# First modulation with a buffer for each weight tile, and the first projections' weights behind them in four large tiles

## The chip, the cores and the metric

The kernel runs on one core of one Trainium2 chip. The metric is the device time of one launch in microseconds; the same program is launched several times and the median of the timed runs is what is compared.

## What is computed

One hybrid decoder block on 512 tokens of 1024 channels, in f32. The change lies in its first lines, `sh1` and `sc1`, and in what follows on them directly:

```python
mod = jax.nn.silu(c) @ w_ada[l] + b_ada[l]                  # (1024) @ (1024 x 6144)
sh1, sc1, gt1, sh2, sc2, gt2 = jnp.split(mod, N_MOD, axis=-1)
h = modulate(rms_norm(x, norm_mix[l]), sh1, sc1)
mix = token_mixer(h, positions, w_in[l], ...)
...
proj = h @ w_in                                             # q_a, kv_a, k_rope | rwkv_in | gate_logits
o_mla = mla_branch(q_a, kv_a, k_rope_raw, positions, ...)   # rotary positions inside
o_rwkv = rwkv7_branch(rwkv_in, ...)
...
x = x + gt1[:, None, :] * mix
h = modulate(rms_norm(x, norm_ffn[l]), sh2, sc2)
x = x + gt2[:, None, :] * peer_ffn(h, w_query[l], ...)
```

## The kernel before

The tokens are worked on in four blocks of 128 (`NB`), in three groups: block 0, block 1, blocks 2 and 3. Each goes through the RWKV projections (`shifted`, weights `w_b`), the recurrent core (`rwkv`), latent attention (`mla_pre`, `mla`, weights `w_a`, `w_u`) and the tail; the expert stage at the end streams all expert weights for blocks 2 and 3 and gathers single experts for blocks 0 and 1. The code is written as streams of steps; a scheduler puts the instructions of all of them into one fixed list for each engine, and each engine works its list strictly in that order. SP's list issues most loads, POOL's the loads `w_a` and `w_u` and the gathers.

Before block 0 can be projected, the first modulation must be known. Lines 342 to 357 make it: the columns `sh1` (i = 0, ends in `hB`) and `sc1` (i = 1, ends in `hA`) are each a sum over eight weight rows `w_ada` of 128x1024, weighted by the condition `sc`. VectorE adds the rows up into `part` (line 348 the first row, line 350 the other seven), eight small matmuls with a column of ones sum `part` over its partitions (`ps_mod`), and lines 354 to 357 add bias and norm. The rows come two in one load of 1 MB (line 344) into a ring of `GL` = 4 buffers, so loads five to eight wait until VectorE is done with the first four. `modulated` then makes the block's `hT` (line 329), on which all of PE's work hangs.

`normed` (lines 277 to 320) scales the block's tokens by their root mean square. `rotary` (lines 387 to 421) makes the sine and cosine tables (`rot`, `cs`, `sn`) with some 45 small VectorE instructions out of `posi` and a constant in `cst`; only attention needs them. `cst` (662.5 KB, the identity and masks) is loaded whole on ACT's queue at the start. `shifted` (line 490 loads, lines 514 and 516 shift) takes each `w_b` tile of 512 KB through a ring `w1` of two buffers. `ada_rows` adds up the other four modulation rows in the same way beside the mixing (`L299`, one instruction for a row of 512 KB), each behind its own load. `kT`, `vA` and `qT2` of attention stand in the `gl` ring behind the weights; `kT` and `qT2` are cleared by POOL (lines 523, 525).

Of the kernel before, what the change touches and what calls it, by code (L numbers as in the profile page):

```python
# [9 lines left out]
F32 = mybir.dt.float32  # L10
# [6 lines left out]
ALU = mybir.AluOpType  # L17
# [15 lines left out]
GL = 4  # L33
# [123 lines left out]
def _build(ctx, tc, nc, A, out):  # L157
# [19 lines left out]
    def bank(name, tag, bufs):  # L177
        return pp.tile([P, 512], F32, name=name, tag=tag, bufs=bufs)
# [57 lines left out]
    def mm(o, l, r, start=True, stop=True):  # L236
        PE.matmul(o, l, r, start=start, stop=stop)  # L237
# [11 lines left out]
    rows = mp.tile([P, NROW], F32, name="rows")  # L249
    posi = cp.tile([P, NB], I32, name="posi")  # L250
    nc.sync.dma_start(cols, A["cols"])
    nc.scalar.dma_start(cst, A["cst"])
    nc.scalar.dma_start(posi, A["pos"])

    def C(k):
# [2 lines left out]
    def col(k):  # L258
        return cols[:, COLS[k][0]:COLS[k][1]]
# [78 lines left out]
    part = [b4("part") for _ in range(2)]  # L338
    V.tensor_scalar(col("ba")[:, 8:], col("ba")[:, 8:], 1.0, None, op0=ALU.add)
    ps = bank("ps_mod", "po", 1)  # L340
    for i in range(2):
        for k2 in range(KT // 2):
            w = pe.tile([P, 2, D], F32, name="w_ada", tag="gl", bufs=GL)
            nc.sync.dma_start(w, A["w_ada"][i, 2 * k2:2 * k2 + 2].rearrange("k p d -> p k d"))
            for k in range(2):
                ck = sc[:, 2 * k2 + k:2 * k2 + k + 1]
                if k2 + k == 0:
                    V.tensor_scalar(part[i], w[:, k], ck, None, op0=ALU.mult)
                else:
                    V.scalar_tensor_tensor(part[i], w[:, k], ck, part[i], op0=ALU.mult, op1=ALU.add)  # L350
        for j in range(8):
            mm(ps[:, 8 * i + j:8 * i + j + 1], part[i][:, j * P:(j + 1) * P], ones)
        if i == 0:
            V.tensor_tensor(hB, ps[:, 0:8], col("ba")[:, :8], op=ALU.add)
        else:
            V.tensor_tensor(hA, ps[:, 8:16], col("ba")[:, 8:], op=ALU.add)
            V.tensor_tensor(hA, hA, col("norm_mix"), op=ALU.mult)

    hTb[0] = modulated(nx0, x0, psum_r)

# [25 lines left out]

    def rotary():
        posf = small("posf", NB)
        V.tensor_copy(posf, posi)
        t5 = u5("rot", [P, 5, n64])  # L390
        ang, rk_, y2, sy, cy = t5[:, 0], t5[:, 1], t5[:, 2], t5[:, 3], t5[:, 4]
        for b in range(NB):
# [95 lines left out]
    def load_w(name, src, w=w2):  # L488
        w = w(name)
        nc.sync.dma_start(w, src)  # L490
        return split(w, k=KT)
# [8 lines left out]
    def shifted(hT, js, make):  # L500
# [2 lines left out]
        c = len(js)  # L503
        ps = psum_w("ps_b")
        for q, j in enumerate(js):
            proj(ps, q * n, load_w("w_b", A["w_b"][j], w1), hT)
        pr = prt("pr", [P, c, n + 1])
        for q, j in enumerate(js):
            G.tensor_copy(pr[:, q, 0:1], carry[:, j:j + 1])
# [978 lines left out]
```

## Time and profile before

| what | value |
|---|---|
| median of 3 runs | 1925.5 us (1922.1 to 1932.53) |
| profiled execution | 1922.58 us |
| its span, first to last instruction | 1920.8 us |
| PE busy | 1719.6 us, 90% of the span |
| DVE busy | 1592.0 us, 83% |
| ACT / POOL busy | 699.4 / 425.4 us |
| PE in the first 50 us | 13.42 us |
| moved by DMA | 588.73 MB, 307 GB/s |

The profiled execution takes 1.8 us more than its span; all times of rows count from the span's start. PE is TensorE, DVE VectorE, ACT ScalarE, POOL GpSimd. An f32 matmul stands in the trace as two instructions, so a projection tile of eight matmuls is 16. "DMA" is the busy share of the core's 16 DMA engines.

### The profile page before, as it was taken

What the parts mean: (1) busy time and instruction counts of PE and PEld (TensorE: products, weight loads), DVE (VectorE), ACT (ScalarE), POOL (GpSimd) and SP (SyncE); (2) the same over time, 40 slices, a digit from 0 to 9 for tenths busy, and PEclk for the clock granted to TensorE, in tenths of its full rate; (3) what the DMA queues carried; (4) which work ended last, traced back from release to release, by engine and by line L of the source; (5) the groups of instructions that cost most, each with busy time, mean ns of one, the idle gap of its engine ahead of it and who ended that gap; (6) DMA issues with size and microseconds to landing.
All of it is one profiled execution on the core that took longest, in us unless ns stands there. A gap on an engine that the chain in (4) does not pass through costs nothing.

```text
span 1920.8 us, 30217 instructions
## 1 busy us (share of the span) xinstructions
PE 1719.6 (90%) x11002; PEld 1469.5 (77%) x11002; DVE 1592.0 (83%) x3655; ACT 699.4 (36%) x1727; POOL 425.4 (22%) x394
## 2 busy tenths in 40 slices
PE   2879999999889999999699979869999999999992
PEld 2667777678888698888388868757899988889992
DVE  6665436359768898888699999979999999999998
ACT  1234232421323232331131133335555555555551
POOL 1210000000322220222232213022332333333233
PEclk9989999999889999999899989979999999999996
DMA  7743755066987875789989879989999999999997
GB/s 301 271 147 121 255 177 188 12 208 200 359 332 251 317 254 197 282 295 362 363 316 351 312 290 320 303 311 404 391 404 415 415 415 413 415 413 415 410 373 281
DMA packets 146065, 588.73 MB, mean 307 GB/s; under 512 B 13806, under 2 KB 41710, under 8 KB 111356
## 3 DMA queue, kind: packets, MB, share of 16 engines
q1 hardware_dynamic: 76336, 284.08, 40.2%
q0 software_dynamic: 39360, 280.51, 37.9%
q10 hardware_dynamic: 30220, 22.22, 3.6%
q8 instruction: 86, 1.41, 0.3%
q14 instruction: 63, 0.52, 0.1%
HBM read 566.81 MB, written 19.94 MB: 305 GB/s over the span
## 4 chain that ended last, share of the span: by engine, by line
PE 34%; issue 30%; DVE 12%; DMA 12%; POOL 11%; ACT 1%; POOLq 0%; ACTq 0%; SPq 0%; DVEq 0%
POOL gl L1134 11%; DMA gl<-in_experts,ii 5%; PE ps_b L237 4%; PE ps_gt L237 4%; DMA w_b<-in_w_b 4%; PE ps_q L237 3%; PE ps_ap L237 2%; PE ps_z L237 2%; DVE acc L1145 2%; DVE gl L1138 2%; PE ps_y L237 2%; PE ps_M L237 1%; PE ps_m L237 1%; PE ps_s L237 1%; PE ps_G L237 1%
## 5 line engine op out<-in xcount | busy, mean ns | idle before, releaser
L1134 POOL DMA_INDIRECT gl<-in_experts,ii x256 | 369.8, 1445 | 1010.5 <-DVE acc L1145 716.2
L1138 DVE SCALAR_TENSOR_TENSOR gl<-gl,h2p 128x1024 f32<-128x1024 f32 x256 | 311.1, 1215 | 51.2 <-DMA gl<-in_experts,ii 50.7
L1145 DVE SCALAR_TENSOR_TENSOR acc<-gl,z,acc 128x1024 f32<-128x1024 f32 x256 | 326.4, 1275 | 12.2 <-ACT z L1140 7.3
L237 PE MATMUL acc<-vl,ch 128*128 128x512 f32 x512 | 204.3, 399 | 6.9 <-DVE vl L1170 6.7
L237 PE MATMUL acc<-vh,cl 128*128 128x512 f32 x512 | 204.2, 399 | 5.6 <-DVE cl L1170 5.4
L237 PE MATMUL ps_z<-hh,ul 128*128 128x256 f32 x704 | 199.4, 283 | 0.2 <-DVE ul L1170 0.2
L237 PE MATMUL ps_z<-hh,uh 128*128 128x256 f32 x704 | 199.5, 283 | 0.0
L237 PE MATMUL ps_z<-hl,uh 128*128 128x256 f32 x704 | 199.2, 283 | 0.0
L237 PE MATMUL acc<-vh,ch 128*128 128x512 f32 x512 | 196.5, 396 | 2.2 <-ACT ch L1169 1.9
L1139 ACT ACTIVATE z<-z 128x1 f32<-128x1 f32 x256 | 51.9, 203 | 367.6 <-DVE gl L1138 366.6
L237 PE MATMUL ps_z<-hf,u_raw 128*128 128x256 f32 x640 | 157.1, 390 | 8.4 <-ACT i1T L1246 8.4
L1170 DVE TENSOR_TENSOR vl<-v_raw,vh 128x1024 fp32r<-128x1024 f32 x128 | 155.9, 1218 | 3.5 <-ACT vh L1169 3.3
L237 PE MATMUL ps_gt<-hT,w_b 128*128 128x128 f32 x1024 | 136.5, 288 | 9.1 <-DMA w_b<-in_w_b 8.8
L237 PEld LDWEIGHTS ps_gt<-hT,w_b 128*128 128x128 f32 x1024 | 127.2, 201 | 15.4 <-DMA w_b<-in_w_b 6.2
L237 PE MATMUL ps_b<-hT,w_b 128*128 128x128 f32 x896 | 126.6, 290 | 13.2 <-DMA w_b<-in_w_b 11.7
L1169 ACT CAST vh<-v_raw 128x1024 fp32r<-128x1024 f32 x128 | 134.1, 1047 | 11.4 <-DMA v_raw<-in_dense 6.3
L237 PEld LDWEIGHTS ps_z<-hl,uh 128*128 128x128 f32 x704 | 135.1, 192 | 3.8
L237 PEld LDWEIGHTS ps_z<-hh,uh 128*128 128x128 f32 x704 | 134.7, 191 | 3.4
L237 PEld LDWEIGHTS ps_z<-hh,ul 128*128 128x128 f32 x704 | 134.7, 191 | 0.4 <-DVE ul L1170 0.4
L237 PEld LDWEIGHTS ps_z<-hf,u_raw 128*128 128x128 f32 x640 | 117.8, 195 | 21.9 <-ACT i1T L1246 8.6
L237 PEld LDWEIGHTS ps_b<-hT,w_b 128*128 128x128 f32 x896 | 115.0, 202 | 24.9 <-issue 13.9
L237 PE MATMUL ps_q<-h2T,w_q 128*128 128x128 f32 x1024 | 125.2, 277 | 1.3 <-DMA w_q<-in_w_query 0.9
(443 smaller groups left out, 3293.4 us busy)
## 6 DMA issues: line engine op xcount, KB each, us to landing
u_raw<-in_dense SPq DMA_DIRECT2D x128, 512.0 KB
v_raw<-in_dense SPq DMA_DIRECT2D x128, 512.0 KB
w_b<-in_w_b SPq DMA_DIRECT2D x90, 512.0 KB
w_q<-in_w_query SPq DMA_DIRECT2D x48, 512.0 KB
w_ada<-in_w_ada SPq DMA_DIRECT2D x32, 512.0 KB
G<-gd SPq DMA_DIRECT2D x13, 1024.0 KB
w_o<-in_w_o SPq DMA_DIRECT2D x24, 512.0 KB
w_out<-in_w_out SPq DMA_DIRECT2D x24, 512.0 KB
```

The lines of the kernel that those rows point to most:

```text
L237: PE.matmul(o, l, r, start=start, stop=stop)
L1134: G.indirect_dma_start(out=gl, out_offset=None, in_=A["experts"], in_offset=bass.IndirectOffsetOnAxis(ap=ii[:, s:s + 1], axis=0))
L1138: V.scalar_tensor_tensor(gl[:, :D], gl[:, :D], 1.0, h2, op0=ALU.mult, op1=ALU.mult, accum_out=z[:, 0:1])
L1139: S.activation(z[:, 1:2], z[:, 0:1], AF.Gelu_apprx_tanh)
L1145: V.scalar_tensor_tensor(acc, gl[:, D:], z[:, 1:2], acc, op0=ALU.mult, op1=ALU.add)
L1169: S.copy(hi, x)
L1170: V.tensor_tensor(lo, x, hi.bitcast(F32), op=ALU.subtract)
```

## The change

```diff
--- before.py
+++ after.py
@@ -249,7 +249,7 @@
     rows = mp.tile([P, NROW], F32, name="rows")
     posi = cp.tile([P, NB], I32, name="posi")
     nc.sync.dma_start(cols, A["cols"])
-    nc.scalar.dma_start(cst, A["cst"])
+    nc.scalar.dma_start(cst[:, :P], A["cst"][:, :P])
     nc.scalar.dma_start(posi, A["pos"])
 
     def C(k):
@@ -338,23 +338,40 @@
     part = [b4("part") for _ in range(2)]
     V.tensor_scalar(col("ba")[:, 8:], col("ba")[:, 8:], 1.0, None, op0=ALU.add)
     ps = bank("ps_mod", "po", 1)
+
+    rows_in = []
+    for _ in range(4):
+        t = pe.tile([P, 2, D], F32, name="w_ada", tag="gl", bufs=GL)
+        rows_in += [t[:, 0], t[:, 1]]
+    rows_in += [hTr("w_ada"), hTr("w_ada"), b4("w_ada"), pe.tile([P, D], F32, name="w_ada", tag="h2p", bufs=1),
+                pe.tile([P, D], F32, name="w_ada", tag="acc", bufs=1), w2("w_ada"), w2("w_ada"), w2("w_ada")]
     for i in range(2):
-        for k2 in range(KT // 2):
-            w = pe.tile([P, 2, D], F32, name="w_ada", tag="gl", bufs=GL)
-            nc.sync.dma_start(w, A["w_ada"][i, 2 * k2:2 * k2 + 2].rearrange("k p d -> p k d"))
-            for k in range(2):
-                ck = sc[:, 2 * k2 + k:2 * k2 + k + 1]
-                if k2 + k == 0:
-                    V.tensor_scalar(part[i], w[:, k], ck, None, op0=ALU.mult)
-                else:
-                    V.scalar_tensor_tensor(part[i], w[:, k], ck, part[i], op0=ALU.mult, op1=ALU.add)
-        for j in range(8):
-            mm(ps[:, 8 * i + j:8 * i + j + 1], part[i][:, j * P:(j + 1) * P], ones)
+        for k in range(KT):
+            w = rows_in[KT * i + k]
+            nc.sync.dma_start(w, A["w_ada"][i, k])
+            if i == 1 and k == KT - 1:
+                for j in range(8):
+                    c = ps[:, 8 * i + j:8 * i + j + 1]
+                    mm(c, part[i][:, j * P:(j + 1) * P], ones, True, False)
+                    mm(c, w[:, j * P:(j + 1) * P], sc[:, k:k + 1], False, True)
+            elif k == 0:
+                V.tensor_scalar(part[i], w, sc[:, k:k + 1], None, op0=ALU.mult)
+            else:
+                marks["ada"] = V.scalar_tensor_tensor(part[i], w, sc[:, k:k + 1], part[i], op0=ALU.mult, op1=ALU.add)
         if i == 0:
-            V.tensor_tensor(hB, ps[:, 0:8], col("ba")[:, :8], op=ALU.add)
-        else:
-            V.tensor_tensor(hA, ps[:, 8:16], col("ba")[:, 8:], op=ALU.add)
-            V.tensor_tensor(hA, hA, col("norm_mix"), op=ALU.mult)
+            for j in range(8):
+                mm(ps[:, 8 * i + j:8 * i + j + 1], part[i][:, j * P:(j + 1) * P], ones)
+    with tc.issue_after(marks["ada"].ins):
+        V.tensor_tensor(hB, ps[:, 0:8], col("ba")[:, :8], op=ALU.add)
+    V.tensor_tensor(hA, ps[:, 8:16], col("ba")[:, 8:], op=ALU.add)
+    V.tensor_tensor(hA, hA, col("norm_mix"), op=ALU.mult)
+    w_first = {}
+    for j in (12, 0, 4, 8):
+        t = pe.tile([P, 2, D], F32, name="w_b2", tag="gl", bufs=GL)
+        nc.sync.dma_start(t, A["w_b"][j:j + 2].rearrange("k p d -> p k d"))
+        for k in range(2):
+            w_first[j + k] = split(t[:, k], k=KT)
+    nc.sync.dma_start(cst[:, P:], A["cst"][:, P:])
 
     hTb[0] = modulated(nx0, x0, psum_r)
 
@@ -386,7 +403,8 @@
 
     def rotary():
         posf = small("posf", NB)
-        V.tensor_copy(posf, posi)
+        with tc.issue_after(marks["ada"].ins):
+            V.tensor_copy(posf, posi)
         t5 = u5("rot", [P, 5, n64])
         ang, rk_, y2, sy, cy = t5[:, 0], t5[:, 1], t5[:, 2], t5[:, 3], t5[:, 4]
         for b in range(NB):
@@ -503,7 +521,7 @@
         c = len(js)
         ps = psum_w("ps_b")
         for q, j in enumerate(js):
-            proj(ps, q * n, load_w("w_b", A["w_b"][j], w1), hT)
+            proj(ps, q * n, w_first.pop(j) if j in w_first else load_w("w_b", A["w_b"][j], w1), hT)
         pr = prt("pr", [P, c, n + 1])
         for q, j in enumerate(js):
             G.tensor_copy(pr[:, q, 0:1], carry[:, j:j + 1])
```

In words: every `w_ada` row of the first modulation has a buffer (eight in the four `gl` buffers, the rest in tiles that are free at that time, three of them the `w2` buffers into which `w_a` is loaded later) and a load of its own of 512 KB; the last row is not added by VectorE but multiplied by eight more matmuls on PE. `hB` is placed behind the last addition. Only the identity part of `cst` (64 KB) is loaded at first, the rest later on SP. The weights `w_b` 12 and 13, 0 and 1, 4 and 5, 8 and 9 (block 0's first projections) are loaded in four loads of 1 MB into the `gl` buffers right behind `w_ada`. The conversion that `rotary` starts with is placed behind the last addition.

What this does to the engines' lists follows. SP's list before, from its start (`hT<-in_x` are tokens of a block):

```order
L251 DMA cols<-in_cols 128x84
L308 DMA hT<-in_x 128x1024
L344 DMA w_ada<-in_w_ada 128x2x1024 x8
L368 DMA rows<-in_rows 128x448
L370 DMA w_up<-in_w_up 128x512
L372 DMA w_gu<-in_w_gate_up 128x512
L374 DMA sk<-in_sk 128x256
L490 DMA w_b<-in_w_b 128x1024 x2
L308 DMA hT<-in_x 128x1024
```

SP's list after, from its start:

```order
L251 DMA cols<-in_cols 128x84
L308 DMA hT<-in_x 128x1024
L351 DMA w_ada<-in_w_ada 128x1024 x16
L371 DMA w_b_190<-in_w_b 128x2x1024
L371 DMA w_b_192<-in_w_b 128x2x1024
L371 DMA w_b_194<-in_w_b 128x2x1024
L371 DMA w_b_196<-in_w_b 128x2x1024
L374 DMA cst<-in_cst 128x1197
L385 DMA rows<-in_rows 128x448
L387 DMA w_up<-in_w_up 128x512
```

The four double `w_b` loads now stand between the last `w_ada` row and `rows`, `w_up`, `w_gu`, `sk`; the loads of line 490 that follow begin eight tiles later in the order of use.

DVE's list before, from the second modulation row to its end (`rot`, `cs` and `sn` are rotary's):

```order
L348 TENSOR_SCALAR part<-w_ada,sc 128x1024
L408 TENSOR_SCALAR rot<-rot 128x64
L420 TENSOR_SCALAR cs<-cs 128x4x16
L350 SCALAR_TENSOR_TENSOR part<-w_ada,sc,part 128x1024
L407 TENSOR_TENSOR rot<-rot 128x64
L421 COPY cs<-cs 128x4x16
L408 TENSOR_SCALAR rot<-rot 128x64
L417 SCALAR_TENSOR_TENSOR sn<-rot 128x4x16
L418 TENSOR_SCALAR sn<-sn 128x4x16
L350 SCALAR_TENSOR_TENSOR part<-w_ada,sc,part 128x1024 x6
L356 TENSOR_TENSOR hA<-ps_mod,cols 128x8
L357 TENSOR_TENSOR hA<-hA,cols 128x8
```

DVE's list after at the same place (line 360 is the old 350, 358 the old 348):

```order
L289 SCALAR_TENSOR_TENSOR rs<-rst,rs 128x1
L360 SCALAR_TENSOR_TENSOR part<-w_ada,sc,part 128x1024
L320 TENSOR_SCALAR hT<-hT,rs 128x1024
L360 SCALAR_TENSOR_TENSOR part<-w_ada,sc,part 128x1024 x5
L358 TENSOR_SCALAR part<-w_ada,sc 128x1024
L360 SCALAR_TENSOR_TENSOR part<-w_ada,sc,part 128x1024 x6
L407 CAST posf<-posi 128x4
L365 TENSOR_TENSOR hB<-ps_mod,cols 128x8
L366 TENSOR_TENSOR hA<-ps_mod,cols 128x8
L367 TENSOR_TENSOR hA<-hA,cols 128x8
```

No rotary instruction stands between the additions any more, `hB` no longer stands between the two halves, and there are 13 long additions in place of 14. In DVE's list after, the rotary instructions now begin behind the r projection's shift (line 534 is the old 516), go around the k projection's shift and `kk`, and end at the v projection's shift and the norm of `kk` (`ssk`):

```order
L532 TENSOR_TENSOR sh<-pr 128x256
L534 SCALAR_TENSOR_TENSOR sh<-sh,cols,pr 128x128 x2
L1077 CAST iota_255<-cst 128x128
L411 TENSOR_SCALAR rot<-cst,posf 128x16 x4
...
L532 TENSOR_TENSOR sh<-pr 128x256
L425 TENSOR_TENSOR rot<-rot 128x64
L534 SCALAR_TENSOR_TENSOR sh<-sh,cols,pr 128x128 x2
L719 TENSOR_SCALAR kk<-sh,cols 128x128 x2
...
L439 COPY cs<-cs 128x4x16
L426 TENSOR_SCALAR rot<-rot 128x64
L532 TENSOR_TENSOR sh<-pr 128x256
L726 TENSOR_SCALAR ssk<-ps_ss 128x4
```

The rows left out there are rotary's, some 45 in all. Behind them, up to the scaled tokens of block 1 (`hT`, the old line 320), DVE's list after has eleven line 299 additions; the list before has seven between the v projection's shift and that same instruction.

PE's list before, from the modulation's matmuls (`ps_b` are block 0's projections, `ps_qa` attention's, `ps_up` the decay's):

```order
L237 MATMUL ps_mod<-ones,part 128x1 x16
L237 MATMUL ps_qa<-w_a,hT 128x416
L237 MATMUL ps_b<-hT,w_b 128x128 x8
L237 MATMUL ps_qa<-w_a,hT 128x416
L237 MATMUL ps_b<-hT,w_b 128x128 x8
L237 MATMUL ps_up<-sh,w_up 128x128 x2
L237 MATMUL ps_qa<-w_a,hT 128x416
L237 MATMUL ps_up<-sh,w_up 128x128 x2
L237 MATMUL ps_qa<-w_a,hT 128x416 x2
L237 MATMUL ps_b<-hT,w_b 128x128 x16
L237 MATMUL ps_qa<-w_a,hT 128x416 x3
```

PE's list after at the same place:

```order
L237 MATMUL ps_mod<-ones,part 128x1 x9
L237 MATMUL ps_mod<-sc,w_ada 128x1
L237 MATMUL ps_mod<-ones,part 128x1
...
L237 MATMUL ps_mod<-sc,w_ada 128x1
L237 MATMUL ps_qa<-w_a,hT 128x416
L237 MATMUL ps_b<-hT,w_b_190 128x128 x8
L237 MATMUL ps_qa<-w_a,hT 128x416
L237 MATMUL ps_b<-hT,w_b_190 128x128 x8
L237 MATMUL ps_qa<-w_a,hT 128x416
L237 MATMUL ps_b<-hT,w_b_192 128x128 x16
L237 MATMUL ps_qa<-w_a,hT 128x416
L237 MATMUL ps_b<-hT,w_b_194 128x128 x16
```

The modulation's sixteen matmuls became 24, the projections run through their first 64 matmuls with little between, and the decay's `ps_up` went behind three of the four double tiles. Further back, attention's first keys and queries of block 0 (`ps_kq` of `w_uq`, `ps_qkT`) moved behind the first steps of the recurrent core, and by PE's 600th of some 8300 instructions the lists agree again to the end.

## Rows read from the trace of the kernel before

**Rows 1.** The page, parts 1 and 2: engines over the span, PE by slice.

```profile
PE 1719.6 (90%) x11002; PEld 1469.5 (77%) x11002; DVE 1592.0 (83%) x3655; ACT 699.4 (36%) x1727; POOL 425.4 (22%) x394
PE   2879999999889999999699979869999999999992
```

**Rows 2.** Stretches of 50 us: columns, the first, one of the last stage.

```profile
core 0: us, PE busy (x) PEld busy (x) DVE busy (x) ACT busy (x) POOL busy (x), PEclk, DMA share, GB/s
0.00:50.00 50.00, 13.42 (x55) 12.13 (x56) 29.36 (x85) 5.72 (x14) 9.29 (x18) 1.00 0.75 289
1450.00:1500.00 50.00, 49.96 (x319) 45.13 (x318) 50.00 (x66) 27.94 (x56) 13.08 (x10) 1.00 1.02 415
```

**Rows 3.** Waits, 0 to 48 us: total, times, longest us.

```profile
ACT hT L329 <- DVE hA L357: 36.5, 1, 36.5
```

**Rows 4.** DMA from 0 to 110 us: GB/s in 40 slices of 2.75 us.

```profile
GB/s 19 384 414 412 408 407 410 410 410 410 349 343 419 264 1 0 110 80 25 243 305 393 399 301 352 247 277 378 240 302 358 252 162 127 398 116 317 198 133 198
```

**Rows 5.** Timeline of the first modulation: start, us, engine, instruction [idle before].

```profile
7.30 0.60 ACT L317 ACTIVATE ps_sqr<-hT 128x512 f32<-128x512 f32 x1 [2.91 <-DMA hT<-in_x]
12.28 0.75 DVE L348 TENSOR_SCALAR part<-w_ada,sc 128x1024 f32<-128x1024 f32 x1 [1.18 <-DMA w_ada<-in_w_ada]
28.37 0.17 DVE L354 TENSOR_TENSOR hB<-ps_mod,cols 128x8 f32<-128x8 f32 x1 [3.29 <-PE ps_mod L237]
30.79 1.92 DVE L421 COPY cs<-cs 128x64 f32<-128x64 f32 x1
30.84 1.81 POOL L523 MEMSET kT<- 32x2048 f32 x1 [26.42 <-DMA w_ada<-in_w_ada]
33.15 7.88 DVE L350 SCALAR_TENSOR_TENSOR part<-w_ada,sc,part 128x1024 f32<-128x1024 f32 x6
41.09 3.57 PE L237 MATMUL ps_mod<-ones,part 128*128 128x1 f32 x16 [12.75 <-DVE part L350]
45.69 1.75 PE L237 MATMUL ps_qa<-w_a,hT 128*128 128x416 f32 x2 [1.04 <-ACT hT L329]
47.24 3.62 PE L237 MATMUL ps_b<-hT,w_b 128*128 128x128 f32 x16
51.97 1.95 PE L237 MATMUL ps_b<-hT,w_b 128*128 128x128 f32 x16
```

**Rows 6.** Stretch 12.2 to 24.8 us, rotary instructions alone: DVE busy, clock, DMA.

```profile
12.20:24.80 12.60, 3.34 (x22) 1.00 1.03 409
```

**Rows 7.** Stretches after the modulation, columns as in rows 2.

```profile
65.60:69.00 3.40, 3.37 (x16) 3.40 (x17) 1.62 (x11) 0.00 (x0) 0.24 (x2) 0.51 0.95 349
45.60:77.90 32.30, 27.15 (x159) 22.59 (x159) 18.96 (x47) 8.31 (x28) 6.64 (x19) 0.95 0.79 270
77.90:127.40 49.50, 39.18 (x234) 31.58 (x232) 39.65 (x129) 16.13 (x45) 6.62 (x20) 0.93 0.56 185
127.40:183.20 55.80, 51.64 (x314) 40.01 (x315) 27.63 (x104) 22.95 (x71) 5.44 (x15) 0.97 0.38 118
```

**Rows 8.** Waits of PE, 45 to 183 us.

```profile
PE ps_b L237 <- DMA w_b<-in_w_b: 8.1, 4, 2.7
PE ps_qa L237 <- DMA w_a<-in_w_a: 1.9, 1, 1.9
```

**Rows 9.** Waits of DVE, 45.6 to 127.4 us.

```profile
DVE part L299 <- DMA w_ada<-in_w_ada: 6.2, 4, 3.2
```

**Rows 10.** Line 299 from 77.9 to 127.4 us: ns min/median/max, starts.

```profile
L299 DVE SCALAR_TENSOR_TENSOR part<-w_ada,sc,part x7: 1267/1276/1285, 79.7 to 124.8; 128x1024 f32<-128x1024 f32 x7
```

**Rows 11.** Three stretches ahead of the v projection's shift: DVE busy, clock, DMA.

```profile
56.30:59.40 3.10, 2.90 (x7) 1.00 0.93 318
65.20:67.60 2.40, 1.99 (x12) 0.57 0.94 317
74.40:76.40 2.00, 1.86 (x9) 1.00 1.03 412
```

**Rows 12.** Timeline of DVE: the v projection's shift.

```profile
77.94 0.43 DVE L514 TENSOR_TENSOR sh<-pr 128x256 f32<-128x256 f32 x1
```

## The prediction

> **What bounds the kernel now.** I read the page first. PE is busy for 90% of the span, and its slices are full except at the very start [rows 1]; in the last stage PE and DVE are busy for nearly the whole of each 50 us and DMA moves 415 GB/s, but in the first 50 us PE works for 13.42 us [rows 2]. Nothing later has an appointed time: what the start loses, everything behind it loses. So I looked at the waits of the start. ACT waits 36.5 us for `hA` before it can make `hT` [rows 3], though DMA moves some 410 GB/s from 5.5 us on [rows 4]. In the timeline DVE gets its first row at 12.28 us, gets `hB` only at 28.37 after 3.29 us idle for PE, does the last six additions in 7.88 us, 1.31 each, PE then multiplies for 3.57 us, and at 45.69 us the first projection begins [rows 5]. DVE is the bound of this stage: besides the rows it carries 22 rotary instructions (3.34 us) between 12.2 and 24.8 [rows 6]. Behind it, PE from 45 to 183 us waits 8.1 us for `w_b` loads and 1.9 for `w_a` [rows 8]. DVE is 80% busy between 77.9 and 127.4 (39.65 of 49.5 us) and half busy around that [rows 7].
>
> **The change part by part.** The times count from the start of the span.
>
> *Loads.* Ahead of the first row stood 42 KB, 662.5 KB of `cst`, 512 KB of tokens, 1248 KB of `w_a` in parallel, and the row comes in a pair of 1 MB: 3.57 MB, which by the slices of [rows 4] had moved at 11.5 us; DVE starts 0.8 later. Now it is 42 + 64 + 512 + 512 KB = 1.16 MB, moved by 5.6 us; with the same 0.8 it lands at 6.4. A further row is 0.524 MB at 410 GB/s, 1.28 us: the fifteenth lands at 24.3, the sixteenth at 25.6. No load waits for DVE any more. The double `w_b` tiles follow by 28, 31, 33 and 36 us, shared with two of `w_a` by 35. The parts of `cst` and `w_up` that come later land by about 42, before their readers.
>
> *DVE.* The tokens land some two microseconds earlier than the 7.30 of [rows 5], so the squares (two of 0.60 with their read-outs) are done at about 6.5 and DVE starts at 6.9. Its list is two first rows at 0.75, thirteen additions at 1.31, nine small instructions of the norm at 0.2 and the scaling, 0.74: 21.0 us, end at 27.9. That is later than the fifteenth row's landing, so DVE remains the bound, by 3.6 us, and a somewhat slower load costs nothing. Against 41.03 it is 13.1 us earlier: 5.4 by the first landing, 3.3 by `hB`, 1.3 by the row given to PE, the rest by rotary.
>
> *The row given to PE.* Sixteen matmuls stand behind the last addition in place of eight: 7.1 us by the 3.57 for eight [rows 5]. It saves an addition of 1.31 and costs 3.57, a loss of 2.3. PE ends at 35.0; with `hB` now behind it, the first projection starts 1.2 us later, 36.2, **9.5 us earlier** than 45.69. If PE's clock rises on the way, up to half of the 7.1 could be saved; bounds 32.7 to 36.2.
>
> *Block 0's projections.* From 45.6 to the v projection's shift at 77.94 [rows 12] it is 32.3 us before. The first 16 instructions of `ps_b` took 3.62 us, the next 16 1.95 [rows 5]: at half speed, 1.2 GHz, as in the stretch at a granted 0.51 [rows 7], though the record shows 1.00 there. I take the same slow 6.2 us at first (two `ps_qa`, 16 `ps_b`), then 112 instructions of `ps_b` at 0.122 less overlap, 13.1, 2.8 of `ps_qa` and `ps_up`, and 0.6 for the copy and shift: 22.7 us, since these tiles are there and the waits of [rows 8] in this part are gone. **9.6 us saved**, 19 in all, shift done at 58.9. Rotary now lies in this part, some 45 instructions of 0.15 us by [rows 6], 7 us; DVE was busy for 18.96 of 32.3 us here [rows 7], much of it the decay's work and `L299`, which now come later, and it waits for projections in between. I cost it at nothing; without that cover it is 7 us.
>
> POOL's three clears of `kT` and `qT2` come in this part too. Beside one of them, 1.81 us, a copy of 64 elements took 1.92 us on DVE [rows 5]; three would hold DVE for at most 5.4. DVE has room for that here, so I cost it at nothing too.
>
> *What is given back.* From 77.94 to block 1's scaled tokens at 127.3, DVE's list grows. Of what was done before the v projection's shift, three pieces now come after it: the decay's scan and reciprocal (2.90 us busy), the key norm of attention with one product (1.99), and attention's scaled keys (1.86) [rows 11]; three of rotary's (0.4) and four more `L299` at 1.28 [rows 10] as well: 12.3 us. So 39.65 busy becomes 51.9. With no idle time it is 51.9, with the 9.85 idle of before 61.8; I take half, 57, since a fuller engine idles less but the chain of norms, PE and back stays: **7.5 us lost** on 49.5, bounds 2.4 to 12.3. Behind that, to 183 us, two heads of attention more are left (2.2 us of PE) and the wait for `w_a` (1.9) falls away, as those loads are issued earlier; 28 us of DVE are free there [rows 7]. From there the lists are the same and everything shifts.
>
> **Sum.** 9.5 + 9.6 - 7.5 - 0.3 = 11 us. On the profiled execution's 1922.58 that is 1911.6. The median of the runs is 2.9 higher, so I say 1914.5.
>
> *A rule on load sizes.* In the last stage weights come in loads of 512 KB too, and DMA moves 415 GB/s there [rows 2]. The Trainium skill, "DMA: Bandwidth & Descriptors", section Bandwidth, wants loads of at least 1 MiB and gives 341 GB/s for a single one of that size; at that rate (my estimate from that page) the sixteenth row would land at 29.5 us and cost 1.5 of the gain. No run here shows a single load by itself; the row with many in flight speaks against a loss.
>
> **The rivals.**
>
> *Most of it stays.* DVE idles little between the shift and block 1 (51.9 us, 5 more kept) and PE's clock is up early (3.5): 19 to 20 us, 1905. For it speaks that DVE idles 9.85 us there now; against it, that PE and DVE answer each other in that stretch.
>
> *The lead is given back.* DVE's longer list has the idle time of before (61.8 us, 4.8 less) and rotary or the clears meet the k projection's shift (up to 7): 0 to 6 us left, 1922. What speaks for it is that DVE is the fullest engine there and that `L299` additions stand ahead of the second norm in its list.
>
> *Late rows.* If the rows came at 243 GB/s, as one slice of [rows 4] shows, a row would take 2.16 us, the sixteenth would land at 38.8, PE would begin the projections at about 46 and the start's lead would be gone; then 9.6 - 7.8 = 2 us remain: 1923. The slices at the time of these loads are at 410, and that one is from later, so this is unlikely.
>
> *Slower.* `L299` stands in DVE's one list and each waits for its own load, which SP issues behind loads that wait for PE. Before, four waits cost 6.2 us, the longest 3.2 [rows 9]. Eleven now stand where DVE is full. At 3.2 each it takes four to eat the 11 us and seven (22 us) to end over 0.5% slower, about 1937. That is double the rate of before.
>
> **Chances and range.** Forecast (gain 6 to 15) 0.58; most stays 0.13; given back 0.15; late rows 0.05; slower 0.09. Half a per cent, 9.6 us, is about what a measurement of this kernel can tell from no change (the three runs spread over 10 us). Of the forecast's 0.58 some 0.37 lie beyond it. So faster 0.50, same 0.41, slower 0.09. The range goes from the rival with the largest gain, less a little for the spread, 1901, to 1926, where the lead is given back and the spread adds 4; about 0.15 to 0.2 is left outside.
>
> **What would show it.** In the changed profile: the first row's product at about 7 us, additions back to back to about 28, `ps_mod` with 32 instructions in 5 to 7 us, the first `ps_qa` near 36; no PE wait for `w_b` until the first group's last tiles; the v projection's shift near 59, block 1's scaling near 116, and from PE's attention to block 1 on a constant lead. Wrong would be: the additions waiting for loads, rotary between k's projection and its norm holding PE, `L299` waits over 6 us, or a lead that shrinks behind 183 us.

## The result and the profile after

The changed kernel takes 1907.93 us (median; 1900.54 to 1917.77) against 1925.5. The ratio is 0.9926, interval 0.9898 to 0.9954: 0.74% or 14 us faster (the two medians lie 17.6 us apart). The forecast was 1914.5 us, with faster by over half a per cent as the likeliest case. The profiled execution has a span of 1906.2 us, 14.6 less than before.

The page and two stretches of 50 us, which answer to [rows 1] and [rows 2]:

```profile
PE 1720.0 (90%) x11018; PEld 1472.0 (77%) x11018; DVE 1587.9 (83%) x3654; ACT 699.8 (37%) x1727; POOL 437.2 (23%) x394
PE   5879999999899999999699979779999999999992
```

```profile
0.00:50.00 50.00, 27.41 (x153) 24.99 (x154) 25.64 (x56) 7.26 (x19) 10.33 (x29) 1.00 0.99 387
1450.00:1500.00 50.00, 50.00 (x323) 45.61 (x322) 49.62 (x65) 28.35 (x56) 18.83 (x10) 1.00 1.02 415
```

PE does twice the work of before in the first 50 us; the last stage is what it was. The start in the timeline, as [rows 5], with the v projection's shift [rows 12] and the scaling of block 1:

```profile
6.65 0.74 DVE L358 TENSOR_SCALAR part<-w_ada,sc 128x1024 f32<-128x1024 f32 x1
11.84 6.56 DVE L360 SCALAR_TENSOR_TENSOR part<-w_ada,sc,part 128x1024 f32<-128x1024 f32 x5
27.05 0.59 PE L237 MATMUL ps_mod<-ones,part 128*128 128x1 f32 x2 [5.01 <-DVE part L360]
34.07 0.17 DVE L365 TENSOR_TENSOR hB<-ps_mod,cols 128x8 f32<-128x8 f32 x1 [7.00 <-PE ps_mod L237]
35.12 1.75 PE L237 MATMUL ps_qa<-w_a,hT 128*128 128x416 f32 x2 [1.08 <-ACT hT L329]
36.67 3.18 PE L237 MATMUL ps_b<-hT,w_b 128*128 128x128 f32 x16
39.68 0.86 PE L237 MATMUL ps_qa<-w_a,hT 128*128 128x416 f32 x2
56.66 0.41 DVE L532 TENSOR_TENSOR sh<-pr 128x256 f32<-128x256 f32 x1
112.00 0.75 DVE L320 TENSOR_SCALAR hT<-hT,rs 128x1024 f32<-128x1024 f32 x1
```

No addition waits for a row. The first projection begins at 35.12 instead of 45.69, the shift comes at 56.66 instead of 77.94, the scaling begins at 112.0 instead of 126.6: leads of 10.6, 21.3 and 14.6 us. The scaling before:

```profile
126.57 0.75 DVE L320 TENSOR_SCALAR hT<-hT,rs 128x1024 f32<-128x1024 f32 x1
```

DMA in 40 slices of 2.75 us, as [rows 4], moves 407 to 423 GB/s while the 512 KB rows come, up to some 27 us, and 383 to 420 behind them up to 41 us, with the double tiles:

```profile
GB/s 81 337 423 413 410 413 414 407 407 408 420 399 413 408 383 406 397 417 335 27 6 52 259 341 285 334 343 204 195 310 73 0 159 68 123 191 0 193 308 191
```

Waits of PE from 35 to 171 us ([rows 8]) and one of DVE from 36 to 125 ([rows 9]):

```profile
PE ps_qkT L631 <- DVE qk L627: 8.0, 1, 8.0
PE ps_b L237 <- DMA w_b<-in_w_b: 3.7, 2, 2.1
PE ps_ss L237 <- ACT sq L720: 2.4, 1, 2.4
```

```profile
DVE part L299 <- DMA w_ada<-in_w_ada: 2.1, 2, 1.1
```

The waits for weights have shrunk from 8.1 us to 3.7, but a single wait of 8.0 for attention's q, which DVE makes, is new. What stands around it (columns as in [rows 2]):

```profile
56.66:112.00 55.34, 39.60 (x219) 30.83 (x218) 47.24 (x159) 15.57 (x46) 7.79 (x21) 0.84 0.53 181
112.00:170.80 58.80, 55.04 (x333) 43.01 (x334) 32.61 (x113) 25.92 (x79) 4.95 (x15) 0.95 0.42 139
108.00:112.00 4.00, 0.00 (x0) 0.00 (x0) 3.98 (x12) 0.00 (x0) 0.00 (x0) 0.50 0.28 114
112.00:116.00 4.00, 3.77 (x17) 3.39 (x18) 1.43 (x4) 1.72 (x4) 0.00 (x0) 0.50 0.38 131
```

The granted clock is 0.50, 1.2 GHz, at the end of that wait and for the 4 us of work behind it. In the whole stretch from shift to scaling its mean is 0.84; before it was 0.93 [rows 7].

**Where the lead goes.** I take two marks: A, the first `ps_qa`, and T, the first `ps_tok` of the later group (183.1 us before, 170.8 after), behind which PE's lists of before and after differ in seven rows only, and from some 230 us in none. T before and after:

```profile
183.10 0.27 PE L758 MATMUL ps_tok<-cst,AR 128*128 128x128 f32 x1
```

```profile
170.84 0.28 PE L776 MATMUL ps_tok<-cst,AR 128*128 128x128 f32 x1
```

A is 10.57 earlier, T 12.3. From A to T:

```profile
45.69:183.10 137.41, 117.86 (x705) 94.08 (x706) 86.24 (x280) 47.20 (x143) 18.69 (x53) 0.95 0.54 178
```

```profile
35.12:170.80 135.68, 116.18 (x700) 92.73 (x701) 90.22 (x327) 47.52 (x142) 21.89 (x56) 0.91 0.53 184
```

The first row is of before, the second of after. PE idles 19.5 us in both: one wait took the other's place. Up to the shift PE, idle for 5.1 us before, now never is; from the shift to T it idles 5.0 us more than before and works 4.0 us more (first row after, up to the shift; then before and after from the shift to T):

```profile
35.12:56.66 21.54, 21.54 (x150) 18.89 (x151) 10.38 (x57) 6.03 (x19) 9.15 (x21) 1.00 0.82 315
```

```profile
77.94:183.10 105.16, 90.67 (x548) 71.49 (x547) 67.28 (x233) 38.98 (x116) 12.01 (x35) 0.95 0.46 149
```

```profile
56.66:170.80 114.14, 94.64 (x552) 73.84 (x552) 79.85 (x271) 41.49 (x125) 12.74 (x36) 0.90 0.48 159
```

Behind T the lead over before, by the same ACT instruction in both traces, goes to 8.2 us at 280, 11.2 at 400, 12.6 at 1000 and 14.8 at the end. One place of this drift is taken up below; the rest isn't explained.

### The profile page after: what moved, and what is told of

Read it like the earlier page. It is cut to its first block, busy times and chain, and to the rows that moved or that the text cites. A ratio compares the mean times of both kernels' runs of the same rounds, so it can differ in the third digit from the quotient of the medians.

```text
span 1906.2 us, 30258 instructions
## 1 busy us (share of the span) xinstructions
PE 1720.0 (90%) x11018; PEld 1472.0 (77%) x11018; DVE 1587.9 (83%) x3654; ACT 699.8 (37%) x1727; POOL 437.2 (23%) x394
## 3 DMA queue, kind: packets, MB, share of 16 engines
q1 hardware_dynamic: 76544, 284.69, 40.4%
## 4 chain that ended last, share of the span: by engine, by line
issue 31%; PE 31%; DVE 13%; POOL 12%; DMA 11%; ACT 1%; POOLq 0%; SPq 0%; ACTq 0%; DVEq 0%
POOL gl L1152 12%; DMA gl<-in_experts,ii 5%; PE ps_b L237 4%; PE ps_gt L237 4%; DMA w_b<-in_w_b 3%; PE ps_q L237 3%; DVE acc L1163 3%; PE ps_z L237 2%; DVE gl L1156 2%; PE ps_ap L237 2%; PE ps_y L237 1%; PE ps_m L237 1%; PE ps_G L237 1%; PE ps_M L237 1%; PE ps_s L237 1%
## 5 line engine op out<-in xcount | busy, mean ns | idle before, releaser
L1152 POOL DMA_INDIRECT gl<-in_experts,ii x256 | 382.9, 1496 | 989.1 <-DVE acc L1163 697.0
L1163 DVE SCALAR_TENSOR_TENSOR acc<-gl,z,acc 128x1024 f32<-128x1024 f32 x256 | 326.6, 1276 | 12.6 <-ACT z L1158 7.1
## 6 DMA issues: line engine op xcount, KB each, us to landing
G<-gd SPq DMA_DIRECT2D x13, 1024.0 KB, 10.6
```

The source lines that it names most:

```text
L1152: G.indirect_dma_start(out=gl, out_offset=None, in_=A["experts"], in_offset=bass.IndirectOffsetOnAxis(ap=ii[:, s:s + 1], axis=0))
L1163: V.scalar_tensor_tensor(acc, gl[:, D:], z[:, 1:2], acc, op0=ALU.mult, op1=ALU.add)
```

## The experiments

Each was run with the kernel before on the same chip; the ratio is to that. The edits are to the changed kernel, unless said otherwise.

**e1_vrow, the last row back on VectorE.**

```diff
-            if i == 1 and k == KT - 1:
-                ... (the 16 matmuls)
-            elif k == 0:
+            if k == 0:
...
-        if i == 0:
-            for j in range(8):
+        for j in range(8):
```

> The changed kernel with the last modulation row added by VectorE again (14 long additions, 16 small matmuls in all). Theory (the row given to PE is a loss on the path that sets the end of the modulation): one addition more, 1.3 us, and eight matmuls less, 3.4 us, so the first ps_qa begins at 33.0 us instead of 35.1, the v projection's shift comes at 54.5 instead of 56.7, and the end is about 2 us earlier. Rival (TensorE's clock decides): the longer run of small matmuls is what lets the clock rise early in the projections; then the first ps_qa still begins at 33.0, but the low clock lasts as much longer, the shift comes at 56 to 57 and the end does not move. Second rival (the last row is late): the last addition waits for its load, and the first ps_qa begins at 35 or later.

```profile
29.19 3.58 PE L237 MATMUL ps_mod<-ones,part 128*128 128x1 f32 x16 [6.36 <-DVE part L355]
```

The first `ps_qa` begins at 33.85 (35.12 after; 35.9 in e4_late299, which has the same start and ran on this chip). So the row on PE does cost 1.3 to 2 us there. But the ratio is 0.9973 (0.9946 to 1.0), slower than the changed kernel's. The small edit also reordered all lists: PE's agrees with that of the changed kernel only from its 1157th instruction on, some 380 us in. The end can't be put down to the row alone; e6_vrow_cst was made for that.

**e2_ring, without the double tiles.**

```diff
-    for j in (12, 0, 4, 8):
+    for j in ():
```

> The changed kernel without the four double weight tiles: the first projections' weights go through the ring of two buffers as before. Theory (the projections were waiting for their weights): the first ps_qa stays at 35 us, the v projection's shift comes 9 to 10 us later, at 66, PE waits for w_b again (6 us or more up to there), and of this up to 6 us comes back by block 1's scaling, since VectorE does the decay's work in the longer wait; the end is 4 to 9 us later. Rival (the projections were short of clock, not of weights): the shift comes within 3 us of 56.7 and the end within 3 us of the changed kernel.

First `ps_qa` 35.63, scaling 124.5, ratio 0.9967 (0.9941 to 0.9992), some 8 us behind the changed kernel, as the theory said. The v projection's shift comes at 71.59 and not at 66:

```profile
71.59 0.42 DVE L532 TENSOR_TENSOR sh<-pr 128x256 f32<-128x256 f32 x1
```

That is 14.9 us late; of this 2.4 has come back at the scaling (12.5 late) and 4.0 at T (10.9 late). From A to T:

```profile
35.63:181.70 146.07, 126.56 (x705) 100.39 (x706) 93.03 (x322) 47.12 (x143) 16.57 (x53) 0.87 0.52 177
```

PE idles 19.5 us again. Its busy time for the same matmuls is 10.4 us more than in the changed kernel, at a mean clock of 0.87.

**e3_rot, constants whole at the start and rotary early.**

```diff
-    nc.scalar.dma_start(cst[:, :P], A["cst"][:, :P])
+    nc.scalar.dma_start(cst, A["cst"])
...
-    nc.sync.dma_start(cst[:, P:], A["cst"][:, P:])
...
-        with tc.issue_after(marks["ada"].ins):
-            V.tensor_copy(posf, posi)
+        V.tensor_copy(posf, posi)
```

> The changed kernel with the constants loaded whole at the start and the rotary tables placed where the scheduler puts them, as before. Theory (VectorE bounds the modulation): 0.6 MB more ahead of the first row, 1.5 us, and 22 or more rotary instructions of 0.15 us between the additions, 3.3 us or more, so the first ps_qa begins at 40 us (39 to 42) and the v projection's shift at 61.5, as rotary lay beside the projections without cost; nothing of it comes back later, and the end is 4 to 5 us later. Rival (rows bound the modulation, rotary lies in the waits): first ps_qa at 36.6 or less, the end within 2 us. Second rival (rotary beside the projections did cost): the stretch from first ps_qa to the shift becomes shorter than 21.5 us by 2 us or more and gives that back.

First `ps_qa` at 41.63, 5.7 later than in e4_late299, as expected, and the shift at 62.37: rotary beside the projections was free. The ratio is 1.0036 (1.0011 to 1.0062), some 21 us behind the changed kernel and not 4 to 5. As in e1_vrow, PE's list differs up to some 380 us, so how much of this loss is rotary's isn't shown.

**e4_late299, the additions of line 299 behind block 1's scaling.**

```diff
-        V.scalar_tensor_tensor(part, w, sc[:, k:k + 1], part, op0=ALU.mult, op1=ALU.add)
+        with tc.issue_after(marks["x1"].ins):
+            V.scalar_tensor_tensor(part, w, sc[:, k:k + 1], part, op0=ALU.mult, op1=ALU.add)
...
-        V.tensor_scalar(x, x, rs, None, op0=ALU.mult)
+        marks[f"x{b}"] = V.tensor_scalar(x, x, rs, None, op0=ALU.mult)
```

> The changed kernel with all line 299 additions held behind the scaling of block 1's tokens: eleven of 1.28 us (14 us) leave VectorE's stretch between the v projection's shift (56.7) and that scaling (112.0) and come behind it, where VectorE is a little over half busy. Theory (VectorE's list is the bound of this stretch and is what gave back 6 of the 21 us): the scaling comes 7 us earlier, at 105 (103 to 108), PE's wait for attention's q (8.0 us) shrinks by 2.5 us or more; the end is 3 to 7 us earlier, if the stretch behind has room for the 14 us. Rival (the stretch is a chain through PE and ACT, and the additions lie in its gaps): the scaling stays within 2 us of 112 and the end too. Second rival (it only moves the load): the scaling is earlier, but the lead is gone by 220 us and the end is the same or later.

The scaling comes at 102.9, 9 us earlier, and PE's wait for q is 5.8: VectorE's list is what holds that stretch. But the ratio is 0.9959 (0.9935 to 0.9983). Behind it the additions then stand ahead of other work and wait for their own loads; waits of DVE up to 260 us, from 103 in e4_late299 and, second, from 112 in the changed kernel:

```profile
DVE part L300 <- DMA w_ada<-in_w_ada: 30.5, 11, 6.3
```

```profile
DVE part L299 <- DMA w_ada<-in_w_ada: 21.0, 9, 4.6
```

The second rival: the load was moved, and the lead over the changed kernel is gone by 160 us. Here too PE's list differs, from 66 to some 380 us. By the same ACT instructions the two profiles then stay within some 5 us of each other, either way, and are level at 1000 us; the 8.5 us of loss at the end of this profile come behind, where the lists agree, and their cause isn't shown. Of the 14.2 us that e1_vrow's profile loses on the changed kernel's, 10 come behind 1000 us in the same way.

From here on I chose edits whose lists stay those of the changed kernel from about PE's 600th instruction on.

**e5_posf, the hold on rotary's first conversion taken away.**

```diff
-        with tc.issue_after(marks["ada"].ins):
-            V.tensor_copy(posf, posi)
+        V.tensor_copy(posf, posi)
```

> The changed kernel with rotary's first conversion (4 elements) no longer held behind the last addition; the engines' lists stay as they are but for that one instruction, which moves ahead. It is at the same time a second look at the changed kernel, on the chip of the runs sent with it. Theory (the start is what it is because of the constants' late load, not because of this hold): first ps_qa within 0.5 us of 35.1, shift at 56.7, scaling of block 1 at 112, and 0.7% faster than before (0.4 to 1.1). Rival (the hold keeps rotary out of the additions): rotary instructions stand between the additions again and the first ps_qa comes at 38 or later.

First `ps_qa` 35.24, shift 56.24, scaling 111.2, T 169.4; ratio 0.9925 (0.9899 to 0.9952). The hold does nothing, and the result stands a second time.

**e6_vrow_cst, the last row on VectorE and the constants ahead of the tiles.** The edit of e1_vrow, and

```diff
+    nc.sync.dma_start(cst[:, P:], A["cst"][:, P:])
     for j in (12, 0, 4, 8):
...
-    nc.sync.dma_start(cst[:, P:], A["cst"][:, P:])
```

> The changed kernel with the last modulation row added by VectorE again, as in e1_vrow, and the rest of the constants loaded ahead of the four double weight tiles instead of behind them; with that the engines' lists agree with those of the changed kernel from TensorE's 350th instruction on, which those of e1_vrow do not before the 1150th. Theory (e1_vrow lost behind the start because its lists differ from 60 to 330 us, not because of the row): first ps_qa at 33 to 33.9, and 1.5 to 2 us of that lead are still there at 300 us; the end 0 to 3 us ahead of e5_posf on the same chip. Rival (the row on TensorE pays later, by the clock or because VectorE is late with rotary): the lead is gone by block 1's scaling, and the end is 3 us or more behind e5_posf, as e1_vrow was behind the changed kernel.

```profile
33.48 3.11 PE L237 MATMUL ps_qa<-w_a,hT 128*128 128x416 f32 x4 [1.27 <-DMA w_a<-in_w_a]
```

`ps_qa` begins 1.76 us earlier than in e5_posf, which ran on this chip, with a wait of 1.27 that a load ends. The shift is 0.6 earlier, the scaling 4.4 later, T 4.0 later (173.4; mean clock 0.89 from A to T); ratio 0.9931 (0.9901 to 0.9961). So the rival holds up to T: the lead at the start is gone. At the end the two can't be told apart, where the rival had a loss of 3 us or more. What e1_vrow lost more (0.9973, the intervals overlap) goes with its other lists; the constants' place differs too.

**e7_bufs, the buffers alone**: the edits of e1_vrow, e2_ring and e3_rot together.

> Of the change only the buffer for every modulation row: the last row is added by VectorE, the constants are loaded whole at the start, rotary stands where the scheduler puts it, and the projections' weights go through the ring of two. Theory (the parts add up, and what the projections wait for decides): first ps_qa at 38.7 (38 to 40.5), 7 us ahead of before; no double tiles, so the v projection's shift at about 68 and block 1's scaling at 125, since the stretch behind the shift gives back what is not weights; the end 0 to 5 us ahead of before (ratio 0.9975 to 1.0). Rival (the buffers are the change): the lead of 7 us is there at 300 us and the ratio is 0.9955 or less. Second rival (nothing but the preloaded weights reaches the end): ratio 0.999 to 1.002.

First `ps_qa` 40.36, shift 74.05, only 3.9 us ahead of before. But T is at 170.6, as early as with the whole change, and the ratio is 0.9957 (0.9932 to 0.9981). My sum for it was wrong on the far side of the shift:

```profile
40.36:170.60 130.24, 113.73 (x704) 89.15 (x705) 84.93 (x280) 47.55 (x143) 19.41 (x53) 0.97 0.54 188
```

PE waits 7.3 us for weights, at most 3.1 at a time for anything else, and from 76 us to T its granted clock never falls.

**e8_double, eight matmuls more behind the last addition.**

```diff
-                    mm(c, w[:, j * P:(j + 1) * P], sc[:, k:k + 1], False, True)
+                    mm(c, w[:, j * P:(j + 1) * P], sc[:, k:k + 1], False, False)
+                    mm(c, w[:, j * P:(j + 1) * P], zc, False, True)
```

> The changed kernel with eight matmuls more behind the last addition: the last row's product is followed by the same row times a column of zeros, so that the sum stays what it is. All lists stay the same but for these. Theory (TensorE's part of the modulation lies on the path that everything behind waits for): first ps_qa 3.4 us later than in e5_posf, shift, scaling and the instructions at 300 us later by 3.4 as well (3 to 3.8), the end too. Rival (the stretch behind has slack): at block 1's scaling less than half of the 3.4 us is left, and the end is within 1.5 us of e5_posf. Second rival (clock): the longer run of matmuls lifts the clock earlier, so the first ps_b tiles are faster and the v projection's shift is later by 2 us or less.

`ps_qa` begins at 38.75, 3.5 us after e5_posf; shift 4.4 later, scaling 4.3, T 4.1 (173.5). The start is on the path up to 200 us, with all lists the same. Near 210 us e5_posf loses about 4 us behind a late weight load (granted clock 0.61 from 208 to 212, 1.00 in e8_double); from there the two profiles differ by no more than 2.6 us either way, and e8_double's ends 0.9 us earlier. The ratio of 0.9938 (0.9915 to 0.9961) is 2.5 us worse, within the intervals: whether the 3.5 us reach the end isn't shown.

**e9_tiles, buffers and double tiles**: the edits of e1_vrow and e3_rot.

> Two parts of the change: the buffer for every modulation row (as in e7_bufs) and the four double weight tiles; the constants whole at the start, rotary early, the last row added by VectorE. From TensorE's 360th instruction on the lists are those of e7_bufs. Theory (a lead at the v projection's shift is lost again where TensorE then waits for VectorE's list and its clock falls): first ps_qa at 40.4 as in e7_bufs, shift at 62 instead of 74, but the first ps_tok of the later group, at 170.6 in e7_bufs and 170.8 in the changed kernel, comes at 167 to 171, with granted clock below 0.9 between shift and block 1's scaling; the end within 4 us of e7_bufs. Rival (the weights' wait is worth its size): first ps_tok at 160 or earlier, the end 8 us or more ahead of e7_bufs.

The shift comes at 61.5, 12.5 us before that of e7_bufs. T comes 13.2 us after it, at 183.8, and the ratio is 0.999 (0.9964 to 1.0015; its interval and that of e7_bufs overlap): up to T the tiles take away all that the buffers gave. The theory expected T at 167 to 171, so the lead lost again, but not the 13 us beyond it. PE's lists of the two differ in order up to 154 us. From A to T, a part of it, and PE's longest waits in it:

```profile
39.60:183.80 144.20, 122.74 (x704) 97.76 (x705) 83.86 (x280) 47.37 (x143) 22.32 (x56) 0.88 0.46 161
```

```profile
66.70:124.10 57.40, 40.04 (x182) 30.43 (x180) 41.97 (x137) 14.31 (x42) 5.97 (x16) 0.76 0.47 165
```

```profile
PE ps_qkT L623 <- DVE qk L619: 8.2, 2, 8.0
PE ps_rsT L723 <- DVE rst L284: 5.7, 1, 5.7
PE ps_b L237 <- DMA w_b<-in_w_b: 2.9, 2, 1.4
```

**e10_late, buffers, later constants and rotary**: the edits of e1_vrow and e2_ring.

> Two parts of the change: the buffer for every modulation row (as in e7_bufs) and the later constants and rotary tables; no double tiles, the last row added by VectorE. Theory (rotary beside the projections is free only as long as these come ahead of it; with the ring of two buffers it comes before the decay's work and pushes that back): first ps_qa at 33.5, 7 us ahead of e7_bufs, but the first ps_tok of the later group at 178 to 182, as in e2_ring (181.7) and not as in e7_bufs (170.6), with a granted clock near 0.8 between shift and block 1's scaling; the end 2 us or more behind e7_bufs. Rival (leads add up): first ps_tok at 165, the end 4 us or more ahead of e7_bufs.

`ps_qa` 33.4, T 172.4, ratio 0.9942 (0.9917 to 0.9967). Neither theory: 7 us of lead at the start come to nothing at T (1.8 behind e7_bufs), but it is not e2_ring's 181.7, from which, of the edits, only the row on VectorE parts it (PE's lists differ in order up to 100 us).

**e11_fill, matmuls of no use in the wait for q.**

```diff
                 ps = psum_m("ps_qkT")
+                if b == 0 and n == 1 and h4_ == 0:
+                    for _ in range(4):
+                        mm(ps, ident, C("mM"))
```

> The changed kernel with four matmuls of 128x512 whose result nobody reads, placed into TensorE's list ahead of the transposes of attention's second q, where it waits 8.0 us for VectorE (104.2 to 112.2); all lists else the same. Theory (behind that wait TensorE works at half clock, 112 to 117.5, and that costs 2.7 us): the fillers take 3.4 us of the wait, the clock falls later or not at all, and first ps_tok of the later group comes 1 to 3 us earlier than in the changed kernel measured against its scaling of block 1 (58.8 us from the one to the other). Rival (4.6 us of idle are left and are enough for the clock to fall): the granted clock behind the wait is 0.5 as before and the 58.8 us stay within 0.5. Second rival (fillers are work): everything behind comes 3 us later.

From scaling to T it takes 56.3 us instead of 58.8, which the theory asked for. But the scaling came at 114.0, two later (VectorE's list had changed in some 20 rows after all, block 1's norm back), and T is at 170.3, ratio 0.9932 (0.9897 to 0.9968). The wait that is left, and that of the changed kernel:

```profile
112.62 1.94 PE L634 MATMUL ps_qkT<-cst,qk 128*96 128x128 f32 x8 [4.51 <-DVE rs L282]
```

```profile
112.23 1.91 PE L631 MATMUL ps_qkT<-cst,qk 128*96 128x128 f32 x8 [8.03 <-DVE qk L627]
```

The clock still fell behind the 4.5 us, but for 3.4 us (112.3 to 115.7) instead of 10.2 (107.5 to 117.7). Counted from the end of the wait, T comes 0.9 us sooner (57.7 us instead of 58.6). In the ratio nothing is gained that can be measured.

**e12_hold, the same in the wait for the squares.**

```diff
         ps = psum_r("ps_ss")
+        for _ in range(3 if cts == (2, 3) and not yTs.get(1) else 0):
+            mm(ps, ident, C("mM"))
```

> The changed kernel with three matmuls of 128x512 whose result nobody reads, placed in TensorE's list ahead of the second pair's ps_ss, where it waits 2.4 us (81.1 to 83.5) for ACT's squares and behind which its granted clock is 0.5 for some 11 us; VectorE's list and all else of TensorE's stay word for word. Theory (the low clock is itself a cost on the path to the first ps_tok of the later group): the clock stays at 1.00 from 84 to 92, ps_v and ps_kq take 1.0 us each instead of 2.1 and 1.9, and that first ps_tok (170.8 in the changed kernel, 169.4 in e5_posf) comes 2 to 5 us earlier. Rival (VectorE's list is the bound there, the low clock only fills TensorE's waiting): the clock stays up too, but TensorE's wait for attention's q grows from 8.0 by what was saved, block 1's scaling stays within 1 us of 112 and the first ps_tok within 1.5 us. Second rival (the 1.6 us of waiting behind ps_ss are enough): the clock falls in the same place and nothing moves, or the fillers delay ps_ss and all is 0.5 to 1 us later.

```profile
84.00:88.00 4.00, 2.78 (x6) 1.32 (x7) 4.00 (x15) 0.48 (x1) 0.00 (x0) 0.67 0.11 26
88.00:92.00 4.00, 4.00 (x14) 2.34 (x13) 1.93 (x10) 2.14 (x6) 1.50 (x2) 0.50 0.45 137
```

The second rival: the clock falls in the same place, behind the 1.8 us wait for `cq`, and `ps_v` takes 2.07 us as before; ratio 0.9945 (0.9921 to 0.9969). T is at 168.9 all the same, 1.9 ahead of the changed kernel. The fillers have no part in it: the lead is there at 79 us, ahead of them. Two places where the lists are the same and only the clock differs, in the changed kernel and then in e12_hold:

```profile
73.21 5.47 PE L237 MATMUL ps_b<-hT,w_b 128*128 128x128 f32 x32 [2.09 <-DMA w_b<-in_w_b]
210.20 5.30 PE L237 MATMUL ps_gt<-hT,w_b 128*128 128x128 f32 x32 [1.99 <-DMA w_b<-in_w_b]
```

```profile
73.10 3.84 PE L237 MATMUL ps_b<-hT,w_b 128*128 128x128 f32 x32 [1.06 <-DMA w_b<-in_w_b]
206.68 3.84 PE L237 MATMUL ps_gt<-hT,w_b 128*128 128x128 f32 x32
```

Behind a load that came one or two microseconds later, the same 32 instructions ran partly at half clock. By the same ACT instructions, e12_hold is 0.9 us late before the first place, 1.7 early after it, and 1.5 to 2.0 from there to 200 us; after the second it is 5.0 early, and at 330 us still 4.9. So a late load and the low clock behind it are passed on for a hundred us and more, as the start is. Not to the end: the 4.9 are 2.7 at 400 us and 0.4 at 1000, as other stretches fall differently.

## Why the prediction was right, and where it was not

The kernels whose lists end alike, in one table. B are the buffers, D the double tiles, L later constants and rotary, R the row on PE; "low" is the time at half clock, twice (1 - mean clock) times the stretch (with the clock unrounded), and behind it the part of that time in which PE works.

| kernel | parts | A | T | PE busy, idle, low (at work) from A to T | ratio |
|---|---|---|---|---|---|
| before | | 45.7 | 183.1 | 117.9, 19.5, 14 (13.1) | 1 |
| e7_bufs | B | 40.4 | 170.6 | 113.7, 16.5, 7 (6.8) | 0.9957 |
| e9_tiles | BD | 39.6 | 183.8 | 122.7, 21.5, 34 (27.4) | 0.9990 |
| e10_late | BL | 33.4 | 172.4 | 120.6, 18.4, 20 (19.1) | 0.9942 |
| e2_ring | BLR | 35.6 | 181.7 | 126.6, 19.5, 38 (33.6) | 0.9967 |
| e6_vrow_cst | BDL | 33.5 | 173.4 | 122.1, 17.8, 31 (27.1) | 0.9931 |
| after | BDLR | 35.1 | 170.8 | 116.2, 19.5, 24 (16.9) | 0.9926 |
| e5_posf | BDLR | 35.2 | 169.4 | 115.7, 18.5, 24 (16.6) | 0.9925 |

The lead at T, from one profile each, is that of the ratio within its interval (e2_ring's at the edge). The intervals are some 10 us wide, and the single profiles drift by up to 7 us behind T, so this is settled there in the main and not to the microsecond. Where the lists are the same (changed kernel, e5_posf, and but for its fillers e12_hold), T itself differs by 1.4 to 1.9 us.

**The modulation: right.** The terms were 9.5 us and measured 10.6: first row at 6.65 (6.9 said), last addition done at 27.0 (27.9), PE's part done by 34.1 (35.0), `ps_qa` at 35.12 (36.2). The row on PE does cost time there, 1.3 to 2 us in e1_vrow and e6_vrow_cst where I said 2.3. That the start is passed on held in e8_double up to 200 us.

**Block 0's projections: right at their place.** 9.6 us said, 10.7 measured (35.12 to 56.66). The first matmuls were slow for some 4.3 us instead of 6.2. Rotary and the clears cost nothing, as costed: PE is busy for all of the 21.54 us.

**What is given back: nearly the right sum, by parts that were mis-sized.** I said 7.5 us between shift and scaling and 0.3 more behind; measured are 6.7 (56.1 us to the scaling's end, 57 forecast), and 2.3 behind, 9 in all. That DVE's longer list holds PE there is borne out by e4_late299, where the scaling came 9 us earlier without the additions. But DVE was busy 48.0 us to the scaling's end, not 51.9, and idle 8.1, not 5; two errors that cancel are luck. What I had no term for is PE's clock. In the new wait for q and three shorter ones it falls: 24 us of low clock from A to T against 14. Yet 7 of the 24 lie in the waits themselves. PE works in 16.9 us of low clock against 13.1 before, which at half rate is some 2 us more (my estimate), and its busy time from A to T is 1.7 us less. So in the changed kernel the clock is at most a small part of the 9 us; the rest is PE's idle time, which moved from ahead of the shift to behind it, and work that moved with it. It weighs more between other kernels: over the table PE's idle time moves by 5 us and its busy time by 12.8, from e7_bufs to e2_ring, where 31 us more of low clock stand: 0.42 us a microsecond. The Trainium skill, "TensorE: Matmul & The Clock Gate", section HAM oscillation, counts half of the throttled time as lost; these two rows come near it, while the table as a whole follows with exceptions of 2 to 4 us, the changed kernel against before among them.

**Terms that add up: wrong.** I priced the tiles at 9.6 us in a sum. Beside the buffers alone they lose 13 us at T (e9_tiles against e7_bufs); beside all the rest they gain 11 (e2_ring against the changed kernel). The row on PE loses 9 at T in e2_ring against e10_late and gains 2.5 to 3.9 in the changed kernel and e5_posf against e6_vrow_cst (whose constants also come earlier). The price of a part goes with the waits that it leaves behind it and with the clock there. Each part also brings another order of the lists between A and T; no run holds the order fixed, so that the order itself sets the price is a rival that is left.

**A constant lead behind 183 us: wrong in detail.** It went from 12.3 to 8.2 and back to 14.8, with lists that are the same but for the seven rows; a lead that shrinks there was one of my signs of being wrong. 3.4 us of it go at the weight load near 210 us and the low clock behind it. So the profile's 14.6 us are 12.3 up to T, against 11 forecast, and 2.3 of drift that nothing had foreseen. The other 2.9 us by which the median lies below the forecast are those that I had added for the median over the profiled execution: here the two are the same. On the rivals: `L299` cost 2.1 us and not more than before, so "slower" had no part, and "late rows" neither (410 GB/s). Falling short of the Trainium skill's rule on loads of 1 MiB ("DMA: Bandwidth & Descriptors", section Bandwidth) cost nothing with sixteen loads of 512 KB queued. "Most of it stays" would have ended at 1905; the 1907.9 lies between it and the forecast.

**Open.** Why the clock falls in one wait and not in another of the same list isn't settled; e12_hold didn't keep it up, and e11_fill only shortened its fall. How much the clock, the order of the lists and DVE's list each take of a lead up to T stays open, and so does the drift behind it. No run beats the changed kernel measurably: e5_posf is equal, and e6_vrow_cst not to be told from it.

## What to carry to other kernels

A stall that is removed early was worth here, to within some 5 us, what was left of it at the next point where all lists meet again: look for that point, and compare PE's busy and idle time and its clock up to there, not the place of the edit. Price PE's waits behind the edit with the slow work that follows each of them, and test parts in more than one company, since they don't add. Before an experiment is believed, see whether its lists agree with the other kernel's: one addition more reordered PE's list up to 380 us here.

## What the hardware showed unexpectedly

The same lists on the same data ran the same 32 matmul instructions in 3.84 or 5.47 us, behind a load that came 1.06 or 2.09 us late. The first 16 instructions of `ps_b`, at the half rate at first, took 2.64, 2.69, 2.74, 3.18, 3.53 and 3.62 us in six kernels, while the record shows a clock of 1.00 there. A VectorE instruction of 0.22 us (line 669 before, 687 after) took 0.54 beside a POOL clear of 1.80.
